# 512-column weight products as two pieces of 256, with slots and weight buffers at multiples of 2 KB

## The chip, the cores and the metric

One Trainium2 chip, of which the kernel uses one core. The metric is the time of one execution on the device in microseconds (us), the median over the runs. Three runs of the kernel before gave 1457.61 to 1458.34 us, with a median of 1458.29 us.

## What is computed

A two-layer network on one sequence of T = 512 tokens with D = 1024 features, in 32-bit floating point. Each layer projects the normed input with a wide matrix `w_in`, runs three branches on it (a latent attention, a state-space scan in chunks, and an attention over the 128 best keys of each query), merges them through gates, and ends with a gate fed by an embedding `p`:

```python
for i in range(DEPTH):                       # DEPTH = 2
    h = rms_norm(x, norm_g[i])
    (c_q, c_kv, k_rope, gate_a, z, xbc, dt_raw, q_c, k_c, v_c, q_idx, k_idx, w_idx, gate_c,
     merge_logits) = jnp.split(h @ w_in[i], split_at, axis=-1)
    o_a = mla_branch(...) * jax.nn.silu(gate_a)
    o_b = ssd_branch(...)
    o_c = dsa_branch(...) * jax.nn.silu(gate_c)
    g_a, g_b, g_c = jnp.split(jax.nn.sigmoid(merge_logits), N_BRANCHES, axis=-1)
    merged = g_a * (o_a @ w_br_a[i]) + g_b * (o_b @ w_br_b[i]) + g_c * (o_c @ w_br_c[i])
    x = x + merged @ w_out[i]
    x = x + jax.nn.sigmoid(x @ w_ple_gate[i]) * (p[i] @ w_ple[i])
return rms_norm(x, final_norm)
```

## The kernel before

Activations are kept transposed, 128 features on the partitions and the 512 tokens along the row, so one tile of them is 128 x 512 numbers of 4 bytes, 2048 bytes on each partition. Such tiles live in 80 slots (`slot`), which are reused in a ring. Weights arrive in units of 128 x 1024 numbers (`wload`): a DMA on SyncE's queue fills `wr`, ScalarE copies it rounded into `wh` (type float32r), and VectorE writes the rest, `wr - wh`, into `wl`. Activations are split in the same way into a high and a low part. There are three buffers each of `wh` and `wl`, and two of `wr` (WB).

A weight product is written three times (`mm`): high weights by high activations (L235), low weights by high activations (L236) and, in a second loop over the 128-row blocks, high weights by low activations (L243). All of them add into one tile `p` of PSUM with 512 columns. The block of 128 x 128 weights stands still in TensorE's array and 512 columns of activations move through it. For float32r the program holds one instruction, and the trace shows it as a weight load (PEld) and a matmul (PE). The same triple is written out in `three`, the first products of each layer (L680, L681, L684), and in `values` with the roles of weights and activations exchanged (L728 to L730). Other products move 128 to 512 columns too: the index scores (L837, L838), the logits (L776 to L778, L880, L881) and the values of both attentions (L599). They are not issued through `mm`.

The order on TensorE is the order in which the program is written (`manual_schedule`): main generators (attention, top-k, scan) are woven with generators of weight products, a few instructions at a time (`weave`, CHUNK = 4). The order on the other engines is set by a scheduler from priorities and from its own estimate of when each instruction can run. `mm` tiles of PSUM come from a ring of three banks.

At the very end, in layer 1, the last three products of the last gate (`pgate`, m = 5, 6, 7) are already done in two halves of 256 tokens (`layer`, the loop over `half`): the first half moves columns 0 to 255 of each activation slot, the second half columns 256 to 511, by the same weight buffers. In the trace these are the forms 128x256 of L235, L236 and L243.

Where the buffers lie follows from the order and sizes of the pools. Ahead of the slots stand 16384 bytes that the compiler sets aside for dynamic DMA, and the pool `const`. In the built program the slots begin at byte 29248 of each partition or whole slots behind it, which is 576 bytes past a multiple of 2048, and the weight buffers at bytes 195840 to 220416, which is 1280 bytes past one. So a full row of a slot has a multiple of 2048 inside it, at column 368. Columns 0 to 255 of a slot contain none, columns 256 to 511 contain one.

Of the kernel before, what the change touches and what calls it, by code (L numbers as in the profile page):

```python
# [93 lines left out]
NV = _o  # L94
# [64 lines left out]
class Build:  # L159
    def __init__(self, tc, I, out, ctx, dbg=None):  # L160
        self.tc, self.nc, self.I, self.out, self.dbg = tc, tc.nc, I, out, dbg or {}
        pool = lambda name, **k: ctx.enter_context(tc.tile_pool(name=name, **k))
        self.const = pool("const", bufs=1)
        self.slots = pool("slots", bufs=1)
        self.small = pool("small", bufs=6)
        self.wp = pool("wp", bufs=2)
        PS = bass.MemoryType.PSUM
        self.psum = pool("psum", bufs=2, space=PS)
        self.dram = pool("dram", bufs=1, space=bass.MemoryType.DRAM)
        self.free_slots = deque(range(NSLOT))  # L170
        self.todo = deque()
        self.of = {}
        self.n = 0
        self.ahead = 0
        self.fetched = {}
        self.chunk = CHUNK
        self.peak = 0
# [49 lines left out]

    def mm(self, ps, w, off, acts, t=slice(0, T)):
# [4 lines left out]
        for k, (ah, al) in enumerate(acts):  # L233
            c = slice(off + 128 * k, off + 128 * k + 128)
            nc.tensor.matmul(ps[:, t], hi[:, c], ah[:, t], start=k == 0, stop=False)  # L235
            nc.tensor.matmul(ps[:, t], lo[:, c], ah[:, t], start=False, stop=False)  # L236
# [4 lines left out]
        for k, (ah, al) in enumerate(acts):  # L241
            c = slice(off + 128 * k, off + 128 * k + 128)
            nc.tensor.matmul(ps[:, t], hi[:, c], al[:, t], start=False, stop=k == n - 1)  # L243
# [10 lines left out]
    def setup(self):  # L254
# [4 lines left out]
        self.v = c.tile([128, L * NV + 8], F32, name="v")  # L259
        self.hv = c.tile([128, L * 32], F32, name="hv")  # L260
        self.expo = c.tile([128, 4], F32, name="expo")
        nc.gpsimd.memset(self.expo[:], -0.5)
# [405 lines left out]
    def prep(self, l, more):  # L668
# [3 lines left out]
        def three(names):  # L672
# [3 lines left out]
            for some in (slice(0, 2), slice(2, 3)):  # L676
                for k, (ah, al) in enumerate(self.h):
                    c = slice(128 * k, 128 * k + 128)
                    for p, (hi, lo) in zip(ps[some], ws[some]):
                        nc.tensor.matmul(p[:], hi[:, c], ah[:], start=k == 0, stop=False)  # L680
                        nc.tensor.matmul(p[:], lo[:, c], ah[:], start=False, stop=False)  # L681
            for p, (hi, lo) in zip(ps, ws):
                for k, (ah, al) in enumerate(self.h):
                    nc.tensor.matmul(p[:], hi[:, 128 * k:128 * k + 128], al[:], start=False, stop=k == 7)  # L684
# [33 lines left out]
    def values(self, l):  # L718
# [3 lines left out]
        for kb in range(4):  # L722
            ps = self.ps("mm")
            t = slice(128 * kb, 128 * kb + 128)
            for k in range(2):
                ah, al = self.ckv[k]
                w = slice(512 * k, 512 * k + 512)
                nc.tensor.matmul(ps[:], ah[:, t], hi[:, w], start=k == 0, stop=False)  # L728
                nc.tensor.matmul(ps[:], al[:, t], hi[:, w], start=False, stop=False)
                nc.tensor.matmul(ps[:], ah[:, t], lo[:, w], start=False, stop=k == 1)  # L730
# [604 lines left out]
NSLOT = 80  # L1335
LAST = 3
# [38 lines left out]
```

## Time and profile before

| | |
|---|---|
| median of three runs | 1458.29 us |
| the profiled execution | 1460.0 us |
| its span, first to last instruction | 1458.2 us |
| mean granted clock of TensorE | 0.993 of full speed |
| TensorE busy | 1418.0 us, 97% of the span, 7252 matmuls |
| weight loads busy | 1155.9 us, 79% |
| VectorE busy | 1092.3 us, 75% |
| ScalarE busy | 719.1 us, 49% |
| moved by DMA | 162.39 MB, 111 GB/s on average |

The span is the time between the first and the last instruction of one profiled execution, and the time of that execution lies 1.8 us above it. "Busy" of TensorE is not a measure of its pace: matmuls overlap in the trace, one row of the timeline lasting 0.39 us while the next one starts 0.23 us after it. What a product costs is read from the distance between the starts of rows that follow each other, and that distance is called the pitch below.

### The profile page before, as it was taken

What the parts mean: (1) busy time and instruction counts of PE and PEld (TensorE: products, weight loads), DVE (VectorE), ACT (ScalarE), POOL (GpSimd) and SP (SyncE); (2) the same over time, 40 slices, a digit from 0 to 9 for tenths busy, and PEclk for the clock granted to TensorE, in tenths of its full rate; (3) what the DMA queues carried; (4) which work ended last, traced back from release to release, by engine and by line L of the source; (5) the groups of instructions that cost most, each with busy time, mean ns of one, the idle gap of its engine ahead of it and who ended that gap; (6) DMA issues with size and microseconds to landing.
All of it is one profiled execution on the core that took longest, in us unless ns stands there. A gap on an engine that the chain in (4) does not pass through costs nothing.

```text
span 1458.2 us, 20141 instructions
## 1 busy us (share of the span) xinstructions
PE 1418.0 (97%) x7252; PEld 1155.9 (79%) x7252; DVE 1092.3 (75%) x2234; ACT 719.1 (49%) x1367; POOL 145.0 (10%) x140
## 2 busy tenths in 40 slices
PE   6999999998999999999999999999999999999997
PEld 4878877787878777888888788888888777788886
DVE  7668786996888987654565697889888798765444
ACT  7557678525656342432345576632465644343232
POOL 0000000021120221000001000000321023100000
PEclk9999999999999999999999999999999999999998
DMA  7442332433333322443353322332333333244331
GB/s 257 143 128 75 92 98 78 131 105 99 109 106 117 120 85 73 158 151 108 118 172 121 94 74 74 92 104 88 116 109 108 105 117 106 82 137 142 108 95 58
DMA packets 67609, 162.39 MB, mean 111 GB/s; under 512 B 9237, under 2 KB 21653, under 8 KB 67509
## 3 DMA queue, kind: packets, MB, share of 16 engines
q1 hardware_dynamic: 67509, 161.11, 35.2%
q8 instruction: 57, 0.93, 0.3%
q14 instruction: 43, 0.35, 0.1%
HBM read 142.27 MB, written 13.83 MB: 107 GB/s over the span
## 4 chain that ended last, share of the span: by engine, by line
PE 73%; DVE 17%; ACT 3%; issue 3%; DMA 2%; POOL 1%; SPq 0%; POOLq 0%; DVEq 0%; ACTq 0%
PE p L243 20%; PE p L235 19%; PE p L236 19%; DVE wl L225 3%; PE p L599 3%; PE p L560 2%; DVE s L861 2%; DVE s L1031 2%; DVE m L858 2%; DMA s<-cum_d 1%; DVE s L963 1%; ACT wh L224 1%; DVE s L1034 1%; PE p L680 1%; PE p L684 1%
## 5 line engine op out<-in xcount | busy, mean ns | idle before, releaser
L235 PE MATMUL p<-s,wh 128*128 128x512 f32 (+1 forms) x1644 | 653.2, 398 | 8.1 <-ACT wh L224 7.7
L236 PE MATMUL p<-s,wl 128*128 128x512 f32 (+1 forms) x1644 | 640.4, 391 | 1.2 <-DVE wl L225 1.2
L243 PE MATMUL p<-s,wh 128*128 128x512 f32 (+1 forms) x1644 | 428.8, 393 | 0.0
L224 ACT ACTIVATE wh<-wr 128x1024 fp32r<-128x1024 f32 (+2 forms) x214 | 223.5, 1044 | 334.0 <-PE p L243 222.1
L235 PEld LDWEIGHTS p<-s,wh 128*128 128x128 f32 x1644 | 311.6, 190 | 70.2 <-ACT wh L224 7.7
L236 PEld LDWEIGHTS p<-s,wl 128*128 128x128 f32 x1644 | 311.6, 190 | 62.6 <-DVE wl L225 2.6
L243 PEld LDWEIGHTS p<-s,wh 128*128 128x128 f32 x1644 | 301.4, 189 | 61.9 <-issue 2.8
L225 DVE TENSOR_TENSOR wl<-wr,wh 128x1024 fp32r<-128x1024 f32 (+2 forms) x214 | 263.0, 1229 | 109.0 <-ACT wh L224 107.7
L550 ACT ACTIVATE s<-s,m 128x128 f32<-128x128 f32 (+3 forms) x128 | 71.5, 558 | 65.5 <-DVE m L549 65.2
L569 ACT ACTIVATE s<-p 128x256 fp32r<-128x256 f32 (+1 forms) x192 | 65.9, 343 | 57.8 <-PE p L560 29.9
L570 DVE TENSOR_TENSOR s<-p,s 128x256 fp32r<-128x256 f32 (+1 forms) x192 | 71.5, 373 | 14.8 <-ACT s L569 13.4
L878 POOL TENSOR_TENSOR s<-s,s 128x256 f32<-128x256 f32 (+2 forms) x48 | 56.6, 1193 | 141.4 <-DMA s<-bias_d 82.9
L560 PE MATMUL p<-c,s 128*128 128x128 f32 x320 | 56.4, 274 | 6.6 <-DVE s L552 6.6
L560 PEld LDWEIGHTS p<-c,s 128*128 128x128 f32 x320 | 40.7, 141 | 24.0 <-issue 11.2
L1127 DVE SCALAR_TENSOR_TENSOR s<-s,p 128x512 f32<-128x512 f32 x48 | 32.6, 679 | 33.0 <-PE p L243 33.0
L407 ACT ACTIVATE s<-s 128x512 f32<-128x512 f32 (+1 forms) x42 | 25.3, 610 | 64.1 <-DVE s L1094 39.9
L552 DVE TENSOR_SCALAR s<-s,m 128x128 f32<-128x128 f32 (+3 forms) x128 | 52.2, 408 | 2.6
L963 DVE SCALAR_TENSOR_TENSOR s<-p,v,s 128x511 f32<-128x511 f32 (+2 forms) x72 | 53.2, 739 | 0.0
L861 DVE MATCH_REPLACE8 s<-m,s 128x256 f32<-128x256 f32 (+2 forms) x96 | 51.7, 544 | 0.0
L858 DVE MAX8 m<-s 128x8 f32<-128x256 f32 (+2 forms) x96 | 49.3, 549 | 0.0
L250 ACT ACTIVATE s<-s 128x512 fp32r<-128x512 f32 (+1 forms) x58 | 36.2, 624 | 26.5 <-DVE s L642 10.9
L251 DVE TENSOR_TENSOR s<-s,s 128x512 fp32r<-128x512 f32 (+1 forms) x58 | 42.3, 730 | 7.6 <-ACT s L250 7.3
(188 smaller groups left out, 1630.5 us busy)
## 6 DMA issues: line engine op xcount, KB each, us to landing
wr<-in_w_dram SPq DMA_DIRECT2D x204, 512.0 KB, 3.5
s<-cum_d SPq DMA_DIRECT2D x32, 256.0 KB, 3.7
s<-in_x_dram SPq DMA_DIRECT2D x16, 256.0 KB, 5.1
ple_d<-s SPq DMA_DIRECT2D x16, 256.0 KB, 4.3
s<-bias_d SPq DMA_DIRECT2D x16, 256.0 KB, 3.5
s<-ple_d SPq DMA_DIRECT2D x13, 256.0 KB, 2.6
s<-bias_d SPq DMA_DIRECT2D x16, 192.0 KB, 2.5
s<-s SPq DMA_DIRECT2D x44, 64.0 KB, 2.0
```

What stands on the lines that cost most here:

```text
L224: nc.scalar.activation(hi[:, :n], raw[:, :n], AF.Copy)
L225: nc.vector.tensor_sub(lo[:, :n], raw[:, :n], hi[:, :n].bitcast(F32))
L235: nc.tensor.matmul(ps[:, t], hi[:, c], ah[:, t], start=k == 0, stop=False)
L236: nc.tensor.matmul(ps[:, t], lo[:, c], ah[:, t], start=False, stop=False)
L243: nc.tensor.matmul(ps[:, t], hi[:, c], al[:, t], start=False, stop=k == n - 1)
L550: nc.scalar.activation(u[:, :n], u[:, :n], AF.Exp, bias=mx, scale=-1.0, accum_out=sm)
L560: nc.tensor.transpose(tp[:, 128 * kb:128 * kb + 128], u[:, 128 * kb:128 * kb + 128], self.ident)
L569: nc.scalar.activation(h_, src, AF.Copy)
L570: nc.vector.tensor_sub(l_, src, h_.bitcast(F32))
L858: i = nc.vector.max(m8, sc[qt][:, :n])
L861: nc.vector.match_replace(sc[qt][:, :n], m8, sc[qt][:, :n], GONE)
L963: nc.vector.scalar_tensor_tensor(a[:, d:], ps[:, :T - d], w(3 - d), a[:, d:], op0=OP.mult, op1=OP.add)
```

## The change

The pools are opened in another order: a small new pool `front` (896 bytes: the vectors `v` and the constant `expo`, both moved out of `const`), then the slots, the weight buffers, and only then `const` and `small`. The space for dynamic DMA is set to 1024 bytes. In the built program the slots begin at byte 2048 or a whole number of slots behind it, and the weight buffers at bytes 165888 to 194560; all of these are multiples of 2048. Nothing else changes its size.

Every product of `mm`, `three` and `values` goes through the new function `wide`, which issues one matmul for each PIECE = 256 columns. Both pieces name the same weights. Only the first piece of the first block starts the sum.

```diff
--- before.py
+++ after.py
@@ -160,10 +160,12 @@
     def __init__(self, tc, I, out, ctx, dbg=None):
         self.tc, self.nc, self.I, self.out, self.dbg = tc, tc.nc, I, out, dbg or {}
         pool = lambda name, **k: ctx.enter_context(tc.tile_pool(name=name, **k))
+
+        self.front = pool("front", bufs=1)
+        self.slots = pool("slots", bufs=1)
+        self.wp = pool("wp", bufs=2)
         self.const = pool("const", bufs=1)
-        self.slots = pool("slots", bufs=1)
         self.small = pool("small", bufs=6)
-        self.wp = pool("wp", bufs=2)
         PS = bass.MemoryType.PSUM
         self.psum = pool("psum", bufs=2, space=PS)
         self.dram = pool("dram", bufs=1, space=bass.MemoryType.DRAM)
@@ -225,6 +227,13 @@
             nc.vector.tensor_sub(lo[:, :n], raw[:, :n], hi[:, :n].bitcast(F32))
         return hi, lo
 
+    def wide(self, ps, w, a, t=slice(0, T), first=False, last=False):
+
+
+        for i in range(t.start, t.stop, PIECE):
+            s = slice(i, i + PIECE)
+            self.nc.tensor.matmul(ps[:, s], w, a[:, s], start=first and i == t.start, stop=last, skip_group_check=True)
+
     def mm(self, ps, w, off, acts, t=slice(0, T)):
 
         nc = self.nc
@@ -232,15 +241,15 @@
         n, cost = len(acts), 0
         for k, (ah, al) in enumerate(acts):
             c = slice(off + 128 * k, off + 128 * k + 128)
-            nc.tensor.matmul(ps[:, t], hi[:, c], ah[:, t], start=k == 0, stop=False)
-            nc.tensor.matmul(ps[:, t], lo[:, c], ah[:, t], start=False, stop=False)
+            self.wide(ps, hi[:, c], ah, t, first=k == 0)
+            self.wide(ps, lo[:, c], ah, t)
             cost += 2
             if cost >= self.chunk:
                 yield cost
                 cost = 0
         for k, (ah, al) in enumerate(acts):
             c = slice(off + 128 * k, off + 128 * k + 128)
-            nc.tensor.matmul(ps[:, t], hi[:, c], al[:, t], start=False, stop=k == n - 1)
+            self.wide(ps, hi[:, c], al, t, last=k == n - 1)
             cost += 1
             if cost >= self.chunk or k == n - 1:
                 yield cost
@@ -256,10 +265,11 @@
         self.c = c.tile([128, 928], F32, name="c")
         self.ident, self.tri, self.ones = self.c[:, 0:128], self.c[:, 128:256], self.c[:, 256:384]
         self.cmask = self.c[:, 416:928]
-        self.v = c.tile([128, L * NV + 8], F32, name="v")
+        front = self.front.tile([128, 224], F32, name="v")
+        self.v = front[:, 0:L * NV + 8]
         self.hv = c.tile([128, L * 32], F32, name="hv")
-        self.expo = c.tile([128, 4], F32, name="expo")
-        nc.gpsimd.memset(self.expo[:], -0.5)
+        self.expo = front[:, 220:224]
+        nc.gpsimd.memset(self.expo, -0.5)
         self.ple_prep(0)
         self.prefetch(0, ("ple", 0))
         self.rel_setup()
@@ -677,11 +687,11 @@
                 for k, (ah, al) in enumerate(self.h):
                     c = slice(128 * k, 128 * k + 128)
                     for p, (hi, lo) in zip(ps[some], ws[some]):
-                        nc.tensor.matmul(p[:], hi[:, c], ah[:], start=k == 0, stop=False)
-                        nc.tensor.matmul(p[:], lo[:, c], ah[:], start=False, stop=False)
+                        self.wide(p, hi[:, c], ah, first=k == 0)
+                        self.wide(p, lo[:, c], ah)
             for p, (hi, lo) in zip(ps, ws):
                 for k, (ah, al) in enumerate(self.h):
-                    nc.tensor.matmul(p[:], hi[:, 128 * k:128 * k + 128], al[:], start=False, stop=k == 7)
+                    self.wide(p, hi[:, 128 * k:128 * k + 128], al, last=k == 7)
             return ps
 
         def raw(ps, s, first):
@@ -725,9 +735,9 @@
             for k in range(2):
                 ah, al = self.ckv[k]
                 w = slice(512 * k, 512 * k + 512)
-                nc.tensor.matmul(ps[:], ah[:, t], hi[:, w], start=k == 0, stop=False)
-                nc.tensor.matmul(ps[:], al[:, t], hi[:, w], start=False, stop=False)
-                nc.tensor.matmul(ps[:], ah[:, t], lo[:, w], start=False, stop=k == 1)
+                self.wide(ps, ah[:, t], hi[:, w], first=k == 0)
+                self.wide(ps, al[:, t], hi[:, w])
+                self.wide(ps, ah[:, t], lo[:, w], last=k == 1)
             self.V.append([])
             for g in range(2):
                 v = self.slot(F32R)
@@ -1333,6 +1343,7 @@
 REL = (1, 3, 4, 4)
 WB = (3, 3, 2)
 NSLOT = 80
+PIECE = 256
 LAST = 3
 CHUNK = 4
 FIRST = (("c_kv", 0), ("c_kv", 1), "C")
@@ -1359,7 +1370,7 @@
     import concourse.bacc as _bacc
     from concourse.bass_utils import run_bass_kernel_spmd as _run
 
-    nc = _bacc.Bacc("TRN2", target_bir_lowering=False, num_devices=1)
+    nc = _bacc.Bacc("TRN2", target_bir_lowering=False, num_devices=1, dynamic_dma_scratch_size=1024)
     packed = pack({k: np.asarray(a) for k, a in inputs.items()})
     arrays, I = {}, {}
     for name, a in packed.items():
```

The order of the instructions on TensorE stays as it was, with each wide product written twice. TensorE in layer 0, just ahead of the last logits of the top-k stage: p740, p743 and p749 are PSUM tiles, s599 a query tile, wh747 and wl747 a weight unit. Before:

```order
L243 MATMUL p740_3715<-s88_421,wh738_3709 128x512
L243 MATMUL p740_3715<-s91_426,wh738_3709 128x512
L880 MATMUL p743_3748<-s152_804,s599_2853 128x256
L881 MATMUL p743_3748<-s153_805,s599_2853 128x256
L235 MATMUL p749_3765<-s69_390,wh747_3759 128x512
L236 MATMUL p749_3765<-s69_390,wl747_3760 128x512
```

The same place in the changed program, where every line number has moved by some ten lines and all weight products carry that of `wide`:

```order
L235 MATMUL p740_4731<-s88_471,wh738_4725 128x256 x2
L235 MATMUL p740_4731<-s91_476,wh738_4725 128x256 x2
L890 MATMUL p743_4788<-s152_1022,s599_3581 128x256
L891 MATMUL p743_4788<-s153_1023,s599_3581 128x256
L235 MATMUL p749_4805<-s69_440,wh747_4799 128x256 x2
L235 MATMUL p749_4805<-s69_440,wl747_4800 128x256 x2
```

Each row that had 512 columns is now two instructions of 256, and the rows between them are untouched.

The scheduler places some instructions of VectorE elsewhere. VectorE in layer 0, where the top-k stage ends (L865) and the gates of the scan begin (L909 to L920); wl747 is the low part of the weight unit above, s592 a gate that reads the PSUM tile p729. Before:

```order
L1127 SCALAR_TENSOR_TENSOR s592_2798<-s592_2798,p729_3644 128x512
L225 TENSOR_TENSOR wl747_3760<-wr747_3761,wh747_3759 128x1024
L865 TENSOR_SCALAR s258_1278<-s258_1278 128x256
L865 TENSOR_SCALAR s259_1279<-s259_1279 128x384
L865 TENSOR_SCALAR s260_1280<-s260_1280 128x512
L909 TENSOR_TENSOR s759_3814<-s136_714,hv_76 128x64
```

The changed program, from the last row ahead of the L920 rows (L918 before, L928 now) on:

```order
L928 TENSOR_TENSOR s759_4878<-s759_4878 128x64
L1137 SCALAR_TENSOR_TENSOR s592_3502<-s592_3502,p729_4624 128x512
L930 SCALAR_TENSOR_TENSOR s759_4878<-s759_4878 128x64 x2
L227 TENSOR_TENSOR wl747_4800<-wr747_4801,wh747_4799 128x1024
L930 SCALAR_TENSOR_TENSOR s759_4878<-s759_4878 128x64 x5
L931 SCALAR_TENSOR_TENSOR s759_4878<-s759_4878 128x64
```

wl747 and the gate s592 have moved from ahead of the rows L865 to behind the first two of the seven rows L920. Of VectorE's 2134 instructions in the program 437 have another place, none by more than 14 places, and of ScalarE's 1241 there are 152, none by more than 5.

## Rows read from the trace of the kernel before

**Rows 1.** The page: the span, and busy time by engine.

```profile
span 1458.2 us, 20141 instructions
...
PE 1418.0 (97%) x7252; PEld 1155.9 (79%) x7252; DVE 1092.3 (75%) x2234; ACT 719.1 (49%) x1367; POOL 145.0 (10%) x140
```

**Rows 2.** The page: share of the engines in the chain that ended last.

```profile
PE 73%; DVE 17%; ACT 3%; issue 3%; DMA 2%; POOL 1%; SPq 0%; POOLq 0%; DVEq 0%; ACTq 0%
```

**Rows 3.** TensorE's groups by shape: count | busy us, mean ns | idle before, releasers.

```profile
L235 PE MATMUL p<-s,wh 128*128 128x512 f32 x1596 | 640.0, 401 | 8.1 <-ACT wh L224 7.7 <-ACT s L394 0.3
...
L560 PE MATMUL p<-c,s 128*128 128x128 f32 x320 | 56.4, 274 | 6.6 <-DVE s L552 6.6
...
L599 PE MATMUL p<-s,vc 128*128 128x256 f32 x192 | 33.6, 302 | 2.6 <-DVE s L570 1.5 <-ACT s L569 1.0
...
L680 PE MATMUL p<-s,wh 128*128 128x512 f32 x48 | 19.0, 396 | 0.9 <-ACT s L447 0.5 <-ACT s L394 0.4
...
L235 PE MATMUL p<-s,wh 128*128 128x256 f32 x48 | 13.2, 309 | 0.0
...
L728 PE MATMUL p<-wh,s 128*128 128x512 f32 x16 | 6.5, 407 | 0.4 <-DVE s L251 0.4
```

**Rows 4.** Timeline of TensorE, 620 to 627 us: start, length, line, count.

```profile
620.88 0.39 PE L235 MATMUL p<-s,wh 128*128 128x512 f32 x1
...
624.54 2.00 PE L243 MATMUL p<-s,wh 128*128 128x512 f32 x8
626.37 0.39 PE L235 MATMUL p<-s,wh 128*128 128x512 f32 x1
```

**Rows 5.** Stretches of the timeline rows: us, TensorE busy (instructions), granted clock, DMA.

```profile
620.88:626.37 5.49, 5.49 (x25) 1.00 0.70 228
1427.35:1430.07 2.72, 2.72 (x27) 1.00 0.00 0
1436.42:1439.20 2.78, 2.78 (x15) 0.50 0.00 0
1444.54:1446.42 1.88, 1.88 (x18) 1.00 0.52 179
```

**Rows 6.** Timeline of TensorE, first half of the last gate.

```profile
1427.35 0.28 PE L235 MATMUL p<-s,wh 128*128 128x256 f32 x1
...
1429.16 1.07 PE L243 MATMUL p<-s,wh 128*128 128x256 f32 x8
1430.07 0.28 PE L235 MATMUL p<-s,wh 128*128 128x256 f32 x1
```

**Rows 7.** Timeline of TensorE, second half: at half the clock, then at full.

```profile
1436.42 0.41 PE L235 MATMUL p<-s,wh 128*128 128x256 f32 x1
...
1439.20 0.41 PE L236 MATMUL p<-s,wl 128*128 128x256 f32 x1
...
1444.54 0.28 PE L235 MATMUL p<-s,wh 128*128 128x256 f32 x1
...
1446.42 1.10 PE L243 MATMUL p<-s,wh 128*128 128x256 f32 x8
```

**Rows 8.** Timeline of the weight loads in the first half.

```profile
1427.35 0.19 PEld L236 LDWEIGHTS p<-s,wl 128*128 128x128 f32 x1
1427.46 0.19 PEld L235 LDWEIGHTS p<-s,wh 128*128 128x128 f32 x1
...
1429.05 0.98 PEld L243 LDWEIGHTS p<-s,wh 128*128 128x128 f32 x8
```

**Rows 9.** Timeline of TensorE: four transposes of 128 columns in a row.

```profile
410.55 0.60 PE L560 MATMUL p<-c,s 128*128 128x128 f32 x4
```

**Rows 10.** Timeline of TensorE, 327 to 336 us: two pairs of logits, a wait.

```profile
327.68 0.40 PE L236 MATMUL p<-s,wl 128*128 128x512 f32 x1
...
331.12 0.28 PE L880 MATMUL p<-s,s 128*128 128x256 f32 x1
331.24 0.28 PE L881 MATMUL p<-s,s 128*128 128x256 f32 x1
331.36 1.09 PE L243 MATMUL p<-s,wh 128*128 128x512 f32 x4
335.51 0.30 PE L560 MATMUL p<-c,s 128*128 128x128 f32 x1 [3.07 <-DVE s L552]
```

**Rows 11.** Timeline of VectorE, 319 to 330 us.

```profile
319.24 1.28 DVE L225 TENSOR_TENSOR wl<-wr,wh 128x1024 fp32r<-128x1024 f32 x1
320.44 1.43 DVE L865 TENSOR_SCALAR s<-s 128x256 f32<-128x256 f32 x3
...
328.95 1.26 DVE L920 SCALAR_TENSOR_TENSOR s<-s 128x64 f32<-128x64 f32 x5
```

## The prediction

> **What bounds the kernel now.** I read the page first. TensorE is busy for 1418.0 of 1458.2 us [rows 1], and the chain that ended last runs over it for 73% of the span, over VectorE for 17% [rows 2]. So a shorter or longer step of TensorE shows almost in full, wherever VectorE isn't the one waited for.
>
> Then I read the groups by shape [rows 3]. L235 has 1596 products of 512 columns, and L236 and L243 have as many each; L680, L681 and L684 have 48 each, L728 to L730 have 16 each. These are 3 x (1596 + 48 + 16) = 4980 products that the change cuts in two. What one costs is its pitch, from the timeline of a stretch with nothing else in it [rows 4]: 24 products start between 620.88 and 626.37 us, so 5.49 / 24 = 228.75 ns each, and all together take 4980 x 228.75 ns = 1139 us, 78% of the span. One nanosecond more or less on a wide product is worth 5 us, and this pitch decides everything.
>
> The granted clock there is 1.00 [rows 5], which is 2.4 GHz. With a column each cycle 512 columns would stream in 213.3 ns and 256 in 106.7, so the wide product carries 15.4 ns that aren't columns. The trace has a few weight products of 256 columns, the two halves of the last gate, which use the same weight buffers and instructions as the change will. In the first half 24 of them take 1430.07 - 1427.35 = 2.72 us [rows 6], 113.3 ns each: 6.6 ns over the columns. In the second half, by then at the full clock, 16 take 1446.42 - 1444.54 = 1.88 us [rows 7], 117.5 ns each: 10.8 ns over. The two halves differ in which columns of a slot they move. Columns 0 to 255 contain no multiple of 2 KB, columns 256 to 511 contain one. Just before, at a granted clock of 0.50 [rows 5] (1.2 GHz, where 256 columns need 213.3 ns), 13 products take 1439.20 - 1436.42 = 2.78 us [rows 7], 213.8 ns each. There the excess is gone, although these are second-half columns: it looks like data that arrive a little too slowly for the full clock, at places in the row.
>
> **What the change costs, part by part.**
>
> *Cutting in two, by itself.* With the slots as they lie today a wide product would become 113.3 + 117.5 = 230.8 ns, which is 2.1 ns more than 228.75: 4980 x 2.1 ns = +10 us.
>
> *Moving the slots.* If the 4.2 ns between the halves are the price of the multiple of 2 KB, an aligned slot has it in neither piece, and both cost what the first half costs today: 2 x 113.3 = 226.6 ns, 2.1 ns less than now, 4980 x 2.1 ns = -10 us. No row has a piece that begins at a multiple of 2 KB, so this has two ends. The low one: what is left of the excess may also come from the address (the first half contains a multiple of 1 KB, which an aligned piece doesn't). Four transposes of 128 columns, each with its own weight load, take 0.60 us [rows 9], and less the 0.274 us of the last one [rows 3] that is 0.326 / 3 = 108.7 ns per load and matmul. A piece can hardly be faster, since it loads 128 x 128 weights too: 2 x 108.7 = 217.4 ns, and 4980 x 11.35 ns = -57 us. The high one: the two halves differ for another reason, and pieces run like the second half, 235.0 ns, 4980 x 6.25 ns = +31 us; or like the pair of logits L880 and L881, which take 331.36 - 331.12 = 0.24 us [rows 10], 4980 x 11.25 ns = +56 us. I take the row with the same line, operands and weights and no 2 KB inside, the first half: -10 us.
>
> *Twice the weight loads.* Each piece loads its weights again, 4980 more loads. In the first half the loads start 0.11 us apart, as do the matmuls [rows 6, 8], over 24 in a row without a gap. So they hide behind the piece ahead of them, if barely: the load is what the low end above rests on. If that cover is lost, the pitch goes to the second-half price.
>
> The Trainium skill ("TensorE: Matmul & The Clock Gate", section "Back-to-back issue gap") has a rule against the change: a matmul of N columns costs N / 2.4 + 2.5 ns, so a fixed toll is paid for each. By that page a wide product would go from 215.8 to 218.4 ns, an estimate of 4980 x 2.5 ns = +12 us. The trace disagrees with it at 512 columns, where it measures 228.75 ns [rows 4]: two first-half pieces cost less than one wide product.
>
> *Weight buffers.* They move from 1280 bytes past a multiple of 2 KB to 0. Today one block of weights in four contains such a multiple, and the pitch of the row of 24 [rows 4] covers all four kinds. I see no separate price, and take 0; what there might be lies inside the two ends.
>
> *Other products that move slots.* L599 has 2 x 192 products of 256 columns [rows 3]; logits and scores move slots too. With 120 ns for a logit today [rows 10] and 113.3 for a clean one, the 384 of L599 would save 384 x 6.7 ns = 2.6 us at most. I take -2 us.
>
> *VectorE's new order.* In the top-k stage wl747 now comes behind two of the rows L920. Today it is done at 319.24 + 1.28 = 320.5 us, and TensorE first uses it at 327.68 [rows 10, 11]. With the same work ahead of it, it ends when those two L920 end today, 328.95 + 2/5 x 1.26 = 329.45: TensorE waits 1.8 us. But 3.07 us are lost anyway at 335.51, for VectorE's softmax L552 [rows 10], so most of it is taken from that wait. If that cover were gone it would cost 1.8 us. The same stage of layer 1 has moves of at most 12 places, with no such wait behind them. I take +1 us, with 0 and +4 as ends.
>
> *Sum.* 1460.0 - 10 - 2 + 1 = 1449 us for an execution like the profiled one. That one lies 1.7 us above the median of the runs, so 1447 us.
>
> **The rivals.**
>
> *Deep.* Pieces reach the price of load and matmul in the transposes, 108.7 ns. For it: the excess vanishes at half the clock [rows 7] and the first half, at 113.3 ns, still contains a multiple of 1 KB. Against it: transposes move another kind of data, 128 columns, and no row has a float32r product below 113 ns. Time: 1460.0 - 57 - 2 + 1 - 1.7 = 1400 us.
>
> *A fixed toll.* Addresses do nothing, the halves differ by something of their own, and two pieces cost their mean: 230.8 ns. For it: every piece in the trace carries 6.6 ns or more beside its columns, and the change issues 4980 more of them. Against it: the two halves have the same lines, weights and shapes. Time: 1460.0 + 10 + 1 - 1.7 = 1469 us. The rule of the Trainium skill above would end near it.
>
> *Slower: the load is no longer hidden.* A wide product has 228.75 ns to hide the next load, a piece about half of that. If load and moving rows, now both at multiples of 2 KB, get in each other's way, the piece costs 117.5 ns or more in steady work. The place is every wide product, and it decides from 114.4 ns a piece (half of 228.75). For it: the second half, and the logits at 120 ns [rows 7, 10], whose weights and columns lie in slots at equal distance from a multiple of 512 bytes, as all will. Against it: 113.3 ns with the same weight buffers over 24 products. Time: 1460.0 + 31 + 1 - 1.7 = 1490 us, and 1515 us at the logits' price.
>
> *No effect.* The pieces cost 114.4 ns, or the gain is eaten by VectorE in the top-k stages: within 0.2% of 1458 us.
>
> **How the numbers follow.** My forecast, clean pieces near 113 ns, gets 0.36, for 1439 to 1453 us by itself (pieces of 112.5 to 113.8 ns). Deep gets 0.24, the fixed toll 0.14, the hidden load lost 0.19 (of it 0.05 at the logits' price), no effect 0.07. Faster by over 0.2%, which is about what a measurement of this kernel can tell from no change, is then 0.36 + 0.24 = 0.60; within 0.2% 0.07; slower 0.14 + 0.19 = 0.33. The range runs from the deep case, 1400 us, to the second-half price, 1490 us; the ends beyond leave out some 0.15.
>
> **What the profile of the changed kernel would show.** The pitch of the pieces in the stretch that is all weight products, after 600 us: 113 ns for my forecast, 109 for deep, 115.4 for the toll, 117.5 or more for the lost load. First and second pieces should cost the same if addresses matter, and the two halves of the last gate, which the change doesn't cut, should come out alike, at 113 ns or less: they test the move of the slots alone. Weight loads should number some 12230 (7252 + 4980). The wait for L552 near 335 us should shrink or be replaced by one for wl. I am wrong if pieces differ from 113 by more than 1 ns, or if TensorE idles by 5 us more than its 40 us of today [rows 1].

## The result, and the profile after

The changed kernel takes 1495.28 us (median of 4 runs, 1494.06 to 1498.53), the kernel before 1458.11 us (4 runs). The ratio is 1.0257 with an interval of 1.0241 to 1.0273: the change costs 37 us, and the forecast of 1447 us had the wrong sign. The profiled execution takes 1494.07 us.

The page of the changed kernel, its span and busy times:

```profile
span 1492.3 us, 30157 instructions
...
PE 1460.0 (98%) x12232; PEld 1424.7 (95%) x12232; DVE 1095.5 (73%) x2234; ACT 718.9 (48%) x1367; POOL 147.9 (10%) x140
...
PE 86%; DVE 7%; issue 3%; DMA 2%; ACT 2%; POOL 1%; SPq 0%; POOLq 0%; DVEq 0%; ACTq 0%
PE p L235 72%; PE p L609 3%; PE p L570 2%; DVE wl L227 2%; PE p L1078 1%; DMA s<-cum_d 1%; PE p L400 1%; PE p L1083 1%; ACT wh L226 1%; PE p L786 1%; PE p L788 1%; PE p L787 1%; DMA sin<-rope_d 1%; DVE s L1041 1%; PE p L1016 1%
```

TensorE has the 4980 instructions more that were counted, and is busy 42.0 us longer than before [rows 1], while the span grew by 34.1 us. Its share of the chain rose from 73% to 86%, VectorE's fell from 17% to 7% [rows 2]: part of what the pieces cost went where TensorE used to wait. The second row of the chain says where the rest is: L235, now the one line of all weight products, is 72% of it.

The pitch in a stretch that holds nothing but weight products, 620 to 740 us (columns as in [rows 5], with the weight loads and the other engines between). First the kernel before, then the changed one:

```profile
620.00:740.00 120.00, 120.00 (x526) 98.48 (x525) 63.60 (x79) 39.41 (x51) 0.00 (x0) 1.00 0.40 128
```

```profile
620.00:740.00 120.00, 120.00 (x1002) 120.00 (x1001) 60.34 (x77) 37.50 (x48) 0.00 (x0) 1.00 0.37 128
```

A row lasts up to twice the pitch, so some two of each count began before the stretch. That gives 120 / 524 = 229.0 ns for a whole product, which agrees with [rows 4], and 120 / 1000 = 120.0 ns for a piece, 240.0 ns for two. This window serves below as the ruler for every kernel. The granted clock is 1.00 in both.

The two halves of the last gate, which the change doesn't cut, in the timeline of TensorE:

```profile
1460.83 0.28 PE L235 MATMUL p<-s,wl 128*128 128x256 f32 x1
...
1462.63 1.24 PE L235 MATMUL p<-s,wh 128*128 128x256 f32 x9
...
1478.19 0.28 PE L235 MATMUL p<-s,wl 128*128 128x256 f32 x1
...
1479.99 1.12 PE L235 MATMUL p<-s,wh 128*128 128x256 f32 x8
```

In the first half 15 products take 1462.63 - 1460.83 = 1.80 us, in the second 1479.99 - 1478.19 = 1.80 us: 120.0 ns in both, where they were 113.3 and 117.5 ns [rows 6, 7]. They are equal, as I said they would be if addresses matter, but dear. These products were only moved, not cut, so the cut did not make them slower.

TensorE's largest waits for VectorE in the stages of the top-k, from the view of waits of the changed kernel (total, times, longest):

```profile
PE p L570 <- DVE s L562: 1.4, 2, 0.7
PE p L235 <- DVE wl L227: 1.2, 3, 0.5
```

The softmax, L552 before and L562 now, is waited for 1.4 us instead of 6.6 [rows 3]. TensorE arrives later, and VectorE's order there is another; what each does is taken up under "VectorE's new order" below.

The order of TensorE's instructions is the same in both, so the starts of all rows can be paired, two pieces with their whole product. 4284 wide products stand between two others of their kind. From start to next start they sum to 990.4 us before and 1032.1 us after, 41.6 us more before rounding. All other intervals, the waits among them, sum to 8.0 us less, and the span of the matmuls' starts grows by 33.6 us.

### The profile page after: what moved, and what is told of

Same layout as the page of the kernel before. It is cut to its first block, busy times and chain, and to the rows that moved or that the text cites. A ratio compares the mean times of both kernels' runs of the same rounds, so it can differ in the third digit from the quotient of the medians.

```text
span 1492.3 us, 30157 instructions
## 1 busy us (share of the span) xinstructions
PE 1460.0 (98%) x12232; PEld 1424.7 (95%) x12232; DVE 1095.5 (73%) x2234; ACT 718.9 (48%) x1367; POOL 147.9 (10%) x140
## 3 DMA queue, kind: packets, MB, share of 16 engines
q1 hardware_dynamic: 67509, 161.11, 32.3%
## 4 chain that ended last, share of the span: by engine, by line
PE 86%; DVE 7%; issue 3%; DMA 2%; ACT 2%; POOL 1%; SPq 0%; POOLq 0%; DVEq 0%; ACTq 0%
PE p L235 72%; PE p L609 3%; PE p L570 2%; DVE wl L227 2%; PE p L1078 1%; DMA s<-cum_d 1%; PE p L400 1%; PE p L1083 1%; ACT wh L226 1%; PE p L786 1%; PE p L788 1%; PE p L787 1%; DMA sin<-rope_d 1%; DVE s L1041 1%; PE p L1016 1%
## 5 line engine op out<-in xcount | busy, mean ns | idle before, releaser
L235 PE MATMUL p<-s,wh 128*128 128x256 f32 x6672 | 1114.9, 285 | 8.5 <-ACT wh L226 7.8
L235 PEld LDWEIGHTS p<-s,wh 128*128 128x128 f32 x6672 | 937.4, 192 | 21.0 <-ACT wh L226 7.8
L235 PE MATMUL p<-s,wl 128*128 128x256 f32 x3336 | 675.0, 283 | 1.2 <-DVE wl L227 1.2
L235 PEld LDWEIGHTS p<-s,wl 128*128 128x128 f32 x3336 | 521.8, 192 | 1.9 <-DVE wl L227 1.9
L227 DVE TENSOR_TENSOR wl<-wr,wh 128x1024 fp32r<-128x1024 f32 (+2 forms) x214 | 267.3, 1249 | 116.8 <-ACT wh L226 115.4
L562 DVE TENSOR_SCALAR s<-s,m 128x128 f32<-128x128 f32 (+3 forms) x128 | 52.0, 406 | 2.6
L973 DVE SCALAR_TENSOR_TENSOR s<-p,v,s 128x511 f32<-128x511 f32 (+2 forms) x72 | 53.3, 740 | 0.1
L438 POOL TENSOR_TENSOR m<-m,v 128x4 f32<-128x4 f32 (+1 forms) x10 | 10.8, 1076 | 395.4 <-DVE m L437 395.4
L456 DVE SCALAR_TENSOR_TENSOR s<-s,v,p 128x512 f32<-128x512 f32 x42 | 29.0, 742 | 28.4 <-PE p L445 28.4
L888 POOL TENSOR_TENSOR s<-s,c 128x128 f32<-128x128 f32 x16 | 9.1, 567 | 366.4 <-DMA s<-bias_d 190.3
```

The source lines that it names most:

```text
L227: nc.vector.tensor_sub(lo[:, :n], raw[:, :n], hi[:, :n].bitcast(F32))
L235: self.nc.tensor.matmul(ps[:, s], w, a[:, s], start=first and i == t.start, stop=last, skip_group_check=True)
L562: nc.vector.tensor_scalar(u[:, :n], u[:, :n], rs, None, op0=OP.mult)
L888: nc.gpsimd.tensor_tensor(b[:, :n], b[:, :n], mask, OP.add)
L973: nc.vector.scalar_tensor_tensor(a[:, d:], ps[:, :T - d], w(3 - d), a[:, d:], op0=OP.mult, op1=OP.add)
```

## Experiments

Theory A, when I saw the result: the new address makes the pieces dear. Theory B: a piece can't hide its own weight load, whatever the address. Where a pitch is given without another source it comes from one ruler, the window from 620 to 740 us with its count less two. `split_halves`, `piece128` and `narrow64_128` have other work in that window and are read elsewhere. A kernel whose time stands without an interval ran once; ten runs of one kernel here lie up to 0.5% apart (`weights_1984_512`, 1456.82 to 1463.63 us), so single totals a few us apart say nothing.

### One part alone

Only the cutting, at the old addresses (`split_only`): the changed kernel with the pools and the space for dynamic DMA of the kernel before. Against the changed kernel, in part:

```diff
-        self.front = pool("front", bufs=1)
+        self.const = pool("const", bufs=1)
         self.slots = pool("slots", bufs=1)
+        self.small = pool("small", bufs=6)
         self.wp = pool("wp", bufs=2)
-        self.const = pool("const", bufs=1)
-        self.small = pool("small", bufs=6)
...
```

> The changed kernel's wide function with 256-column pieces, in the pools and at the addresses of the kernel before. Theory A (addresses): the even 120 ns of the changed kernel comes from slots and weights at multiples of 2 KB; here first pieces cost 113.3 ns and second pieces 117.5, as in the last gate of the kernel before, 230.8 ns a pair and some 1468 us. Theory B (weight load): a piece cannot hide its own weight load, which takes 120 ns whatever the addresses; here both pieces cost 120 ns, and the time is that of the changed kernel, 1490 to 1500 us.

Only the new addresses, products whole (`align_only`), against the changed kernel:

```diff
-            s = slice(i, i + PIECE)
+            s = slice(i, min(i + PIECE, t.stop))
...
-PIECE = 256
+PIECE = 512
```

> The changed kernel with PIECE = 512, so that only the addresses differ from the kernel before. Theory A: the aligned addresses cost something here too, a wide product goes from 228.75 to 233 ns or more, which is +21 us or more, 1480 us. Theory B: with 228 ns for a load to hide in, nothing changes but small things, a wide product costs 228 to 229 ns, 1455 to 1462 us. If the crossing of a multiple of 2 KB is a price of its own, it falls to some 224.5 ns and 1440 us.

The old addresses, and all first halves of a PSUM tile ahead of all its second halves (`split_halves`), in part:

```diff
+        for i in range(t.start, t.stop, PIECE):
+            p = slice(i, i + PIECE)
+            for k, (ah, al) in enumerate(acts):
...
+                self.wide(ps, hi[:, c], ah, p, first=k == 0 and i == t.start)
```

> Pieces of 256 at the addresses of the kernel before, but in another order: mm issues all products of columns 0 to 255 of a tile, then all of columns 256 to 511, so that the weights change with each piece and the half stays, as in the last gate of the kernel before. Theory A: stretches of 24 at 113.3 ns and of 24 at 117.5 ns alternate, some 1468 us. Theory B: 120 ns throughout, 1490 to 1500 us. A difference from split_only would say that what counts is loading the same weights twice in a row or jumping between halves.

`split_only`: 1478.51 us, ratio 1.0142 (1.0127 to 1.0158). `align_only`: 1456.24 us, ratio 0.9984 (0.9973 to 0.9995). `split_halves`: 1481.09 us in one run. The same stretch of `split_only`, then of `align_only`:

```profile
620.00:740.00 120.00, 120.00 (x1022) 120.00 (x1021) 61.18 (x77) 37.94 (x49) 0.00 (x0) 1.00 0.38 126
```

```profile
620.00:740.00 120.00, 120.00 (x531) 99.41 (x530) 62.94 (x79) 40.10 (x53) 0.00 (x0) 1.00 0.41 128
```

Cutting alone gives pieces of 120 / 1020 = 117.6 ns, 235.3 ns for two instead of 229.0; alignment alone makes whole products 120 / 529 = 226.8 ns. So the parts cost +20 and -2 us and together +37: they don't add up, and neither A nor B alone is right. With pieces, the move costs 1495.28 - 1478.51 = 17 us; with whole products it gains 2. And the price of first and second halves doesn't differ. In `split_halves` the two runs of halves in the timeline have one pitch, 118 ns:

```profile
637.91 0.28 PE L233 MATMUL p<-s,wh 128*128 128x256 f32 x1
...
638.85 1.22 PE L233 MATMUL p<-s,wh 128*128 128x256 f32 x9
639.91 0.28 PE L233 MATMUL p<-s,wl 128*128 128x256 f32 x1
...
641.68 1.22 PE L233 MATMUL p<-s,wh 128*128 128x256 f32 x9
```

8 products of one half of the columns take 0.94 us, the 9 that follow (8 of that half and the first of the other) 1.06, and 15 of the other half 1.77 us: 117.5 to 118 ns each. A multiple of 2 KB inside a piece costs nothing here.

### Is it the weight load?

If a piece waits for its load, shorter columns should not help and a narrower block of weights should. `piece128` is the changed kernel with PIECE = 128. The four others leave out half or three quarters of the weights' columns:

```diff
-            self.nc.tensor.matmul(ps[:, s], w, a[:, s], start=first and i == t.start, stop=last, skip_group_check=True)
+            q = 128 if first or last else 64
+            self.nc.tensor.matmul(ps[:q, s], w[:, :q], a[:, s], start=first and i == t.start, stop=last, skip_group_check=True)
```

with PIECE 256 (`narrow64`), 128 (`narrow64_128`), 512 (`narrow64_512`), and with PIECE 256 and 32 for 64 (`narrow32`). They leave most of the upper output rows without their sum and serve for timing alone.

> The changed kernel with PIECE = 128: four pieces to a wide product, each with its own weight load, at aligned addresses. The columns of a piece take 53.3 ns, so the pitch is the price of a load and nothing else. Theory B in its plain form: 120 ns a piece, 480 ns a wide product, +1250 us and more, 2700 us. If a load can follow a load in 109 ns, as the transposes of the kernel before show, 436 ns and some 2480 us, and then a load alone does not explain 120 ns for a piece of 256. A fixed toll of 13.3 ns a matmul without a bound by loads would give 67 ns a piece and some 1640 us.

> The changed kernel, in which the weight products load only 64 of the 128 weight columns, apart from the first and last block of each sum; the upper 64 output rows are so left without most of their sum. A load of 64 columns takes about half as long. If the toll of some 13 ns a piece belongs to the matmul itself (each matmul pays it, whatever it hides), the pitch stays 119 to 120 ns and the time 1490 to 1500 us. If a piece waits for its weights (theory B), the pitch falls towards the columns alone, 107 to 112 ns, and the time to 1400 to 1440 us.

> The same with PIECE = 128, four pieces a wide product, with 64 weight columns but for the first and last block; it leaves out the same sums. A load of 128 weight columns bound that piece to 110 to 114 ns at the full clock. With half the load (some 55 ns) a toll of 13.3 ns on the columns' 53.3 gives 67 ns a piece, if the clock stays full. If there is no toll of the matmul's own, it is 55 to 58 ns, the load or the columns. At half the clock about 107 ns in either case, which would tell nothing.

> Wide products whole (512 columns) at aligned addresses, but with only 64 of the 128 weight columns in all but the first and last block of a sum, which leaves out most of the upper 64 output rows. The runs so far fit one formula: pitch = moved columns / 2.4 + weight columns / 9.6 ns, so that a load of 128 weight columns takes 13.3 ns away from the stream and one of 64 takes 6.7. It gives 213.3 + 6.7 = 220.0 ns here, against 226.7 with 128 weight columns. If the toll at 512 columns were of another kind (fixed for the matmul, or of the columns), it would stay at 226 to 227 ns.

> Pieces of 256 at aligned addresses with 32 weight columns in all but the first and last block, which leaves out most of the upper 96 output rows. The formula (columns / 2.4 + weight columns / 9.6) gives 106.7 + 3.3 = 110.0 ns. If 113.3 ns, as with 64 weight columns, is a floor of the matmul and not of the load, it stays at 113 to 114 ns.

`piece128` takes 3622.3 us, far over all three times expected, because the clock fell. Its page has the granted clock by slices, and two of its stretches are these:

```profile
PEclk9999955558999555555555599755559998555555
```

```profile
100.00:200.00 100.00, 100.00 (x902) 99.39 (x901) 33.50 (x55) 29.85 (x49) 4.83 (x7) 1.00 0.22 64
...
1500.00:1600.00 100.00, 100.00 (x471) 100.00 (x470) 11.90 (x14) 7.00 (x10) 0.00 (x0) 0.50 0.09 27
```

At the full clock (2.4 GHz) a piece takes 100 / 900 = 111 ns (some 50 of the 900 rows are other products; the median from start to start is 111 too), at half (1.2 GHz) 100 / 469 = 213 ns, twice the 53.3 and 106.7 ns that its 128 columns need at a column each cycle. With half the columns of weights, in `narrow64_128` below, the pace is 60 ns. So here the weight load sets the pace, and a load of 128 columns of weights takes about as long as 256 columns moving. A piece of 256 has no room to spare behind it; a whole product has.

That makes a late load plausible for the 120 ns. The narrow kernels speak against it as the whole cause:

| kernel | columns of weights, of a piece | us | ns each |
|---|---|---|---|
| the changed kernel | 128, 256 | 1495.28 | 120.0 |
| `narrow64` | 64, 256 | 1460.48 | 114.0 |
| `narrow32` | 32, 256 | 1476.65 | 117.9 |
| `narrow64_128` | 64, 128 | 1755.31 | 60 |
| `narrow64_512` | 64, 512 | 1460.25 | 229.9 |

The values are counts of the ruler, 60 ns from four pieces per 0.24 us in the timeline of `narrow64_128` (expected were 67 with a toll, 55 to 58 without). Half the weights made a piece cheaper (114.0 ns, between the 119 to 120 and 107 to 112 of the two theories), which I took for proof of a toll that grows with the load. A quarter of them made it dearer again. `narrow64`, then `narrow32`:

```profile
620.00:740.00 120.00, 120.00 (x1055) 120.00 (x1054) 63.60 (x80) 39.13 (x50) 0.00 (x0) 1.00 0.39 128
```

```profile
620.00:740.00 120.00, 120.00 (x1020) 110.85 (x1018) 61.06 (x76) 38.17 (x49) 0.00 (x0) 1.00 0.39 125
```

120 / 1018 = 117.9 ns, where my formula wanted 110.0. With 512 columns and half the weights the product was no cheaper (229.9 instead of 220.0). The formula fell. Nor is 117.9 the price of a load of 32 columns: just ahead of the window the same kernel runs at another pace.

```profile
604.25 0.39 PE L236 MATMUL p<-s,wl 128*32 128x256 f32 x2
...
607.20 1.99 PE L236 MATMUL p<-s,wh 128*32 128x256 f32 x16
```

26 pieces take 607.20 - 604.25 = 2.95 us, 113.5 ns each. Both narrow kernels lie below the 120 ns of the full load, so a part of the load in the 120 isn't ruled out; what fell is that its length alone sets the price.

### Distance between weights and slots

The old layout has weights 704 bytes past the slots, counted from multiples of 2 KB; the new one 0. So I moved one against the other, with pieces of 256 first:

```diff
+        self.gap = pool("gap", bufs=1)
...
+        self.gap.tile([128, 16], F32, name="gap")
```

The gap lies between the slots and the weight buffers, 16 numbers for 64 bytes (`weights_64`), 176 for 704, 320 for 1280, 160 for 640, 8 for 32, 496 for 1984. `shift_576` has no gap but a larger `front`, and both 576 bytes past a multiple of 2 KB.

> The changed kernel with everything behind the front pool moved by 576 bytes: slots and weight buffers both at 576 bytes past a multiple of 2 KB, pieces of 256. The split alone, with slots at 576 and weights at 1280, cost mostly 118 ns a piece; the changed kernel, both at 0, cost 120. If the equal distance of rows and weights from a multiple of 2 KB makes 120 of 118 (theory R), this run has 120 and 1495 us. If it is where the slots themselves lie, or the weights themselves (theories S and W), it has 117 to 118 and some 1479 us.

> The changed kernel with the slots at multiples of 2 KB and the weight buffers 1280 bytes past one, pieces of 256. Theory S (slots decide): 120 ns a piece and 1495 us. Theories R and W (equal distance, or the place of the weights, decides): 117 to 118 ns and some 1479 us. Together with the run that moves both by 576 bytes: R alone gives 120 there and 118 here, S 118 there and 120 here, W 118 in both.

> The changed kernel with slots at multiples of 2 KB and weight buffers 704 bytes past one, which is their distance in the kernel before (1280 - 576). Pieces cost 118 ns or 113 with the split alone and 120 in the three layouts with distances 0, 0 and 1280. If the distance between weights and rows is what counts, beyond 128 or 256 bytes alone, this run has 117 to 118 ns and some 1479 us; if it is the old places of the other pools or something else of the old layout, 120 ns and 1495 us.

> As the last, with the weight buffers 64 bytes past a multiple of 2 KB: 704 = 5 x 128 + 64, so a distance of 64 in units of 128 bytes, like the kernel before. If only the place within 128 bytes counts, 117 to 118 ns and some 1479 us; if it needs 704 (the place within 256 or 512 bytes), 120 ns and 1495 us.

> Slots at multiples of 2 KB, weight buffers 640 bytes past one, pieces of 256. 640 is 5 times 128, where 704 (117.7 ns a piece, 1474 us) was 5.5 times. Theory (equal place within 128 bytes locks the pieces): 120.0 ns and 1495 us, like distances 0 and 1280. Rival (it is the distance modulo 512 or 2048 that matters, and 640 is simply another one): 113 to 118 ns and 1468 to 1480 us.

> Slots at multiples of 2 KB, weight buffers 32 bytes past one, pieces of 256: half of the 64 bytes that unlocked the pieces. Theory (only the odd half of a 128-byte line helps): 120.0 ns and 1495 us. Rival (any unequal place within 128 bytes helps): 113 to 118 ns and 1465 to 1480 us.

Then the same gaps with PIECE = 512:

> Slots at multiples of 2 KB, weight buffers 64 bytes past one, and the weight products whole (512 columns). With pieces of 256 this place gave 1469 us where equal distance gave 1495. Theory (how far the weights lie from the moving rows, modulo 128 bytes, sets what a matmul costs beside its columns): whole products should also cost less than the 226.7 ns of the aligned kernel with whole products (1456.2 us); with the 6.6 to 11 ns over the columns that pieces show at this place, 220 to 224 ns, a time of 1425 to 1445 us. Rival (the distance only matters where the next weight load has no time to spare, that is for pieces of 256): no gain, 226 to 230 ns and 1453 to 1460 us.

> Slots at multiples of 2 KB, weight buffers 640 bytes past one, whole products of 512 columns. Measured so far for whole products: 226.7 ns at distance 0, 228.6 at 704, 233.0 at 64. Theory (for whole products the cost grows from distance 0 towards the odd multiples of 64 bytes, the opposite of pieces): 640, a multiple of 128, is as cheap as 0: 226 to 228 ns, 1454 to 1458 us. Rival (no rule by the distance; each layout has its own price): outside of 226 to 228 ns.

> Slots at multiples of 2 KB, weight buffers 32 bytes past one, whole products of 512 columns. Theory (whole products get dearer from distance 0 to 64 as pieces get cheaper): between 227 and 233 ns, 1457 to 1468 us. Rival (no rule by the distance): below 226.5 or above 233.5 ns.

> Slots at multiples of 2 KB, weight buffers 1984 bytes past one, that is 64 bytes ahead of one, whole products of 512 columns. Theory (only the distance within 128 bytes counts): the price of distance 64, 233 ns and 1469 us. Rival (it counts on which side the weights lie, as 704 and 64 differ too): about 228.6 ns and 1458 us, or another price.

All layouts, sorted by their distance modulo 256 bytes, with ns each by the ruler and us in all:

| modulo 256 | distances | whole products | pieces of 256 |
|---|---|---|---|
| 0 | 0, 0 (`shift_576`), 1280 | 226.8, 1456.2 | 120.0, 1495.3; 120.0, 1495.0; 120.0, 1496.7 |
| 32 | 32 | 233.5, 1470.6 | 118.2, 1483.4 |
| 64 | 64 | 233.5, 1469.2 | 117.6 (113.0 in other stretches), 1469.1 |
| 128 | 640 | 233.5, 1472.5 | 118.7, 1489.1 |
| 192 | 704 (before, `split_only`, `weights_704`), 1984 | 229.0, 1458.1; 229.0, 1460.0 | 117.6, 1478.5; 117.6, 1474.1 |

What the reader is to see: absolute addresses don't matter. `shift_576` moved both to 576 and has the changed kernel's count to the row, x1002; so has `weights_1280`. `shift_576`, then `weights_1280`:

```profile
620.00:740.00 120.00, 120.00 (x1002) 120.00 (x1001) 60.36 (x76) 37.51 (x48) 0.00 (x0) 1.00 0.39 129
```

```profile
620.00:740.00 120.00, 120.00 (x1002) 120.00 (x1001) 61.03 (x78) 36.87 (x47) 0.00 (x0) 1.00 0.39 130
```

And distance 1984 at entirely new addresses gives the count of the kernel before:

```profile
620.00:740.00 120.00, 120.00 (x526) 98.46 (x525) 63.25 (x79) 39.12 (x50) 0.00 (x0) 1.00 0.41 127
```

None of the three theories for these two runs allowed 120 ns in both. Weights at 1280 bytes cost 120.0 ns with the slots at 0 (`weights_1280`) and 117.6 with the slots at 576 (`split_only`), so neither place decides alone: the distance does, by less than its 2 KB. `weights_704` and `weights_64` came out at the 117 to 118 ns expected from the distance. My next rule, the distance modulo 128 bytes, did not hold. With pieces, `weights_640` and `weights_32` came out between what theory and rival had said. With whole products `weights_64_512` (233.5 ns) missed both theory (220 to 224) and rival (226 to 230), and `weights_640_512` (233.5 instead of 226 to 228) and `weights_1984_512` (229.0 instead of 233) went against the theory; `weights_32_512` (233.5) lies on the edge between the two. Modulo 256 all layouts of one class agree. That rule was found after the runs, and 32, 64 and 128 stand on one layout each, so it is a description that fits, not a tested law.

The order isn't the same for both lengths: distance 0 is best for whole products and worst for pieces. At 64 cutting costs nothing (1469.2 and 1469.1 us), because there whole products are dear and many of the pieces run at a cheaper pace than the table's, as shown next. `weights_64_512`, meant to beat both kernels, is 1.0072 (1.0055 to 1.0089) of before; `weights_640_512` is 1.0084 (1.0055 to 1.0113), `weights_1984_512` 1.0002 (0.9989 to 1.0016). The best version is `align_only`, the change without its cutting, by 2 us.

One layout has more than one pace. `weights_64` in two stretches, both full of weight products:

```profile
620.00:740.00 120.00, 120.00 (x1022) 120.00 (x1021) 61.07 (x76) 37.83 (x49) 0.00 (x0) 1.00 0.39 127
765.00:785.00 20.00, 20.00 (x179) 20.00 (x178) 12.68 (x18) 8.23 (x14) 1.57 (x2) 1.00 0.30 94
```

117.6 ns in the first, 20 / 177 = 113.0 ns in the second, at one clock. In the timeline the first pace lasts unbroken from 604 to 756 us; then come a few other products and a wait of 0.35 us, and the second pace lasts from 761 to 785. So the pace isn't set by the distance alone. `weights_704`, at the distance of the kernel before, has both too, 117.6 ns in the ruler and 113.0 here:

```profile
765.00:785.00 20.00, 20.00 (x179) 20.00 (x179) 12.38 (x18) 8.61 (x14) 1.58 (x2) 1.00 0.28 94
```

Taken 24 at a time, over all rows of pieces with no other product between them, this gives a share for each pace. The cheaper pace holds in 109 of 249 groups in `weights_64`, in 12 of 251 in `weights_704`, in 1 of 251 in `split_only`, and in none of 254 in the changed kernel, at distance 0. That mixture fits the lower total of `weights_64`, 1469.1 us against 1474.1 for `weights_704`, though the counts in the ruler are the same; each ran once.

## Why the prediction was wrong

- **What bounds the kernel**: right. The weight products decide, though not at 5 us for each ns: by the ruler two pieces are 11 ns dearer than a whole product, and the kernel lost 37 us, 3.4 for each nanosecond.
- **Moving the slots, -10 us**: the step that failed. I put "both cost what the first half costs today", 113.3 ns, because that row had the same line, operands and weights and no 2 KB inside. Measured: 120.0 ns, and with pieces the move costs 17 us instead of gaining 10. The 4.2 ns between the halves weren't the price of a multiple of 2 KB: `split_halves` has one price for both. What fits is two paces of one layout: `weights_704`, at the same distance, holds both inside one kernel, as `weights_64` does, and the 24 rows of one stretch had caught the cheaper. Taken twelve starts at a time, the old gate gives 113.3 ns and later 117.8, and so do the two paces of `weights_704`. At the new distance, 0, the cheaper pace doesn't occur. The products between two others were to lose 2 ns each and gained 41.6 us / 4284 = 9.7 ns.
- **Its bounds**: the price measured was in the text as the high end, "like the pair of logits", 120 ns and +56 us. I gave it 0.05 and left it outside the range. Its reason was good: the logits' weights and columns lie in slots, at distance 0 modulo 512, where all wide products now lie. But that the number fits is luck. I read one pair; the one ahead of it in the kernel before takes 327.44 - 327.22 = 0.22 us, not 0.24:

```profile
327.22 0.28 PE L880 MATMUL p<-s,s 128*128 128x256 f32 x1
...
327.44 0.40 PE L235 MATMUL p<-s,wh 128*128 128x512 f32 x1
```

  Of the 32 such pairs 28 run without a longer stop, and these take 114 to 121 ns a product. A pair between other products is not steady work.
- **Cutting in two, +10 us**: right in sign and half its size. By itself it cost 20 us, at 117.6 instead of the mean of 115.4 ns: the mean counted half of the pieces at the cheaper pace, which `split_only` has in 1 of 251 groups.
- **Twice the weight loads**: that they hide behind the piece ahead, if barely, is not refuted, but barely was no margin to rest -10 us on. Loads are busy 95% of the span; a load of 128 takes as long as 256 columns move (`piece128`). That it is a late load which makes the 120 isn't shown, and `narrow32` speaks against its length as the only cause.
- **The lost-load rival**: right in its place and its condition of equal distance, and by luck in its price; its mechanism was shown only in that the distance decides between the prices of steady pieces. Its 1515 us was too much by 20, since the products beside other work and the waits gave back 8.0 us and not all 4980 products grew by 11.25 ns.
- **The fixed toll**: at distance 0 it describes the numbers: 226.8 ns is 13.5 over the columns, 120.0 is 13.3 over, as if each matmul paid the same and the cut paid it twice. The rule of the Trainium skill ("TensorE: Matmul & The Clock Gate", section "Back-to-back issue gap") has 2.5 ns for what measures 13.3; that section gives it for an isolated matmul and says that in a stream of loads and matmuls both set the spacing, which the prediction left out. At distance 64 a fixed toll doesn't hold: 20.2 ns over for whole products, 6.3 to 10.9 for pieces.
- **Deep**: no group of 24 whole loads and pieces of 256 columns lies under 113 ns in any layout, and loads for 128 columns follow each other at 111 (`piece128`).
- **Other products, -2 us**: nothing. The values, L599 before and L609 now, which were to bring it, follow one another at a median of 119 ns before and 120 after. The logits became dearer: 28 of the 32 pairs take 120 to 121 ns a product, where they took 114 to 121. One pair in the timeline of the changed kernel:

```profile
338.75 0.28 PE L890 MATMUL p<-s,s 128*128 128x256 f32 x1
338.87 0.28 PE L891 MATMUL p<-s,s 128*128 128x256 f32 x1
338.99 0.40 PE L235 MATMUL p<-s,wh 128*128 128x256 f32 x2
```

- **VectorE's new order, +1 us**: no cost seen. The waits for wl are 1.2 us in three pieces, none over 0.5, so the 1.8 us at 327 us didn't come, and that for the softmax shrank by 5.2 us. TensorE idles 32.3 us instead of 40.2, not 5 us more. In the traces `align_only` and `weights_64_512` have VectorE's order of the kernel before, `weights_64` that of the changed kernel. The waits for the softmax in `align_only`, in `weights_64_512` and, at the same total as the latter, in `weights_64`:

```profile
PE p L570 <- DVE s L562: 8.0, 7, 3.6
PE p L572 <- DVE s L564: 5.7, 7, 1.9
PE p L572 <- DVE s L564: 2.7, 4, 1.0
```

  At the old order it shrinks as the products get dearer, from 8.0 over the 6.6 of the kernel before to 5.7 us; the cut with its new order takes 3.0 us more. No run has that order without the cut.

What stays open: how the distance modulo 256 bytes acts, why it ranks 0 best for whole products and worst for pieces, and what picks the pace where a layout has several.

## What to carry to other kernels

Take the price of a new shape from a kernel that does it in steady work, not from one short stretch of the old one: a row of back-to-back matmuls can keep one of several paces, and 24 rows show one. Cutting a wide product in two doubles the number of loads, and at 256 columns the load is about as long as the product (111 and 106.7 ns here); cut only where something else needs it. Where two buffers are read at once in every instruction, vary their distance by 64 bytes or so and measure, once for each length of product.

## What was not expected of the hardware

- The distance between weights and moving columns changed the pitch of whole products between 226.8 and 233.5 ns, of pieces between 117.6 and 120.0 by the ruler, with the same instructions. Two of the distances have stretches of pieces at 113.0. In all that is 16 us of this kernel with whole products (1456.2 to 1472.5) and 28 us with pieces (1469.1 to 1496.7).
- With pieces of 128 columns the granted clock fell to 0.50 for most of the run (mean 0.685), though PE was shown busy for 99% of it and weight loads for 98%, in a row of loads and products without a gap. At half the clock the pace is 213 ns for 128 columns. In `narrow64_128`, with half the weights in each load, the mean clock was 0.964 and the pace 60 ns.
